# Two of eight chunk pairs of two merged down panels multiplied as 2x2 blocks with seven products

## The chip, the cores and the metric

One core of a Trainium2 chip runs the whole kernel. Its engines are TensorE (PE in the profile; its loads of the stationary operand are PEld), VectorE (DVE), ScalarE (ACT), GpSimd (POOL) and SyncE (SP, which issues the loads here). The metric is the device time of one execution in microseconds; the figure given for a kernel is the median of its runs.

## What is computed

A decoder trunk of two layers on 256 tokens of width 2048: a gated linear attention layer, then a forgetting attention layer, each with a memory attention head group and a channel mixer behind it. The change lies in the channel mixers:

```python
def conv_ffn(h, w_up, conv_w, conv_b, w_down):
    u = causal_dwconv(h @ w_up, conv_w, conv_b)
    a, val = split_cols(u, [FFN_HIDDEN, FFN_HIDDEN])
    return (jax.nn.silu(a) * val) @ w_down
```

`FFN_HIDDEN` is 5632, 44 chunks of 128; `w_down` is 5632 x 2048. All is fp32.

## The kernel before

**Precision.** Every fp32 operand is split into a high and a low part in fp32r, a = ah + al, and a product is ah·bh + al·bh + ah·bl, three matmuls. A weight comes as a *unit*: 128 x up to 1024 numbers (512 KB), loaded by SP into `raw`, cast by ScalarE into `whi` (L201), and VectorE subtracts to get `wlo` (L202). `raw`, `whi` and `wlo` have four buffers each. `split_unit` does this under `tc.high_priority(offset=AHEAD)`, AHEAD = 300: the scheduler, which fixes each engine's order when the kernel is built, treats it as if it stood 300 instructions earlier.

**The mixer.** `ffn` (L1186 on) works through three parts of the hidden chunks, `PARTS = ((0, 16), (16, 32), (32, 44))`. In each part the up panels (two chunks of the gate and two of the value each, eight units) are multiplied, their results turned through HBM and run through `convolve`, which leaves the product of SiLU and value in `m[i]`, split in high and low, chunk i as 128 hidden rows x 256 tokens. Then `add_out` multiplies `m` by the part's rows of `w_down`, in four panels f of 512 columns. A unit of a down panel holds two chunks x 512 columns; its 12 matmuls are 2 chunks x 2 token blocks b x 3 products, with 128 tokens of `m` stationary and 512 columns of the weight moving. The two token blocks accumulate in two PSUM banks, which VectorE adds into the residual `x[f]` (L330, `add_to`).

**The order of a part's down panels.** Panels 0 and 1 run through `two_tm`: seven units of panel 0, seven of panel 1, then the last unit of each; panel 1 accumulates in the two banks named `s`, panel 0 in two of the four named `acc`. Between these units the last convolutions are closed. Panels 2 and 3 then run one after the other through `proj_tm` (its matmul is L276), eight units each. Behind parts 0 and 1 follow the next part's up panels, behind part 2 the next stage of the trunk.

PSUM has eight banks here: four `acc`, two `s`, one `t`, one `o`.

Of the kernel before, what the change touches and what calls it, by code (L numbers as in the profile page):

```python
# [20 lines left out]
P = 128  # L21
# [17 lines left out]
NUNIT = 1024  # L39
AHEAD = 300  # L40
WARM = 9

FV_PARTS = ((0, 376), (376, 764), (764, 1152), (1152, 1536))

# [9 lines left out]
def _panels():  # L54

    full = list(range(KC))
    out = []

    def fm(key, w, c0, kcs=full):
        out.append((key, w, kcs, [(c0, 256)], 4))

    def tm(key, w, c0, n, kcs=full, more=()):
        out.append((key, w, kcs, [(c0, n), *more], 2))

    tm(("mv", 0), ("mem_w_kv", 0), 512, 512)
    for l in range(2):
        tm(("mk", l), ("mem_w_kv", l), 0, 512)
    tm(("mv", 1), ("mem_w_kv", 1), 512, 512)  # L70
    tm(("gv", 0), ("gla_w_in", 0), G_V, DV, more=[(G_R, RANK)])
    tm(("mq", 0), ("gla_w_in", 0), G_MQ, 512)
    for h in range(GLA_H):
        tm(("gqk", h), ("gla_w_in", 0), G_Q + h * DK, DK, more=[(G_K + h * DK, DK)])
        if h == GLA_H - 1:
            tm(("og", 0), ("gla_w_in", 0), G_OG, 512)
        if h:
            tm(("gv", h), ("gla_w_in", 0), G_V + h * DV, DV)
    for j in range(1, 3):
        tm(("og", j), ("gla_w_in", 0), G_OG + j * 512, 512)  # L80
    late = list(range(12, 16)) + list(range(12))

    def ffn(l):
        for p, (lo, hi) in enumerate(PARTS):
            for j in range(lo, hi, 2):
                tm(("up", l, j), ("ffn_w_up", l), j * P, 2 * P, more=[(HID + j * P, 2 * P)])
            for f in range(4):
                tm(("down", l, p, f), ("ffn_w_down", l), f * 512, 512, list(range(lo, hi)))

    for f in range(4):  # L90
        tm(("wo", 0, f), ("gla_w_out", 0), f * 512, 512, late)
# [12 lines left out]
    ffn(1)  # L104
    return out
# [30 lines left out]
def _trunk(ctx: ExitStack, tc: tile.TileContext, xt, xtok, memt, wp, wgu, gns, gfin, cnv, par, msk, out):  # L136
# [45 lines left out]
    def work(tag, bufs=1):  # L182
        return pwork.tile([P, 512], F32, name="ps_" + tag, tag=tag, bufs=bufs)
# [99 lines left out]
    def panel_tm(key, src, evac, second=False):  # L283

        units = where[key]
        n = units[0][2]
        base = min(min(u[1]) for u in units)
        acc = []  # L290
        end = len(units) - 1

        def step(i):
            if i == 0:
                acc.extend(work("s", 2) if second else pacc.tile([P, 512], F32, name="acc", tag="acc")
                           for _ in range(2))
            ready = split_unit(units[i])
            passes = [(b, low) for low in range(2) for b in range(2)]
            if i == end:
                passes.sort()  # L300
            for b, low in passes:
                for j, kc in enumerate(units[i][1]):
                    for part in range(2 - low):
                        mm = TE.matmul(acc[b][:, :n], src[kc - base][:, part, b * P : (b + 1) * P],  # L304
                                       ready[low][:, j * n : (j + 1) * n], start=i == low == part == j == 0,
                                       stop=i == end and low == 1 and j == len(units[i][1]) - 1)
                if i == end and low:
                    ends.append(mm)
                    evac(b, acc[b][:, :n])
            last_mm.append(mm)  # L310

        return step

    def run(step, hooks={}, count=8):

# [199 lines left out]
    def halves(dst, src):  # L515
        S.activation(dst[0], src, AF.Copy)
        V.tensor_tensor(dst[1], src, dst[0].bitcast(F32), ALU.subtract)
# [634 lines left out]
                    steps[f](u)  # L1152


    def add_out(key, src, then=None, spare=None, last=None, first=0, hooks=None, late=1):
# [13 lines left out]
        for f in range(first, 4):  # L1169
# [10 lines left out]
    def ffn(l, nx, h, m, ys, zs, landing, then, spare=None, last=None):  # L1180
        with tc.tile_pool(name=f"ffn{l}", bufs=1) as fp:
            cw = fp.tile([P, 4 * 88], F32, name="cw")
            nc.sync.dma_start(cw, cnv[l])
# [4 lines left out]
            count = [0, 0]  # L1188
            open_ = []

            def convolve(j, i, z):

                for s in range(2):
                    cv = {}
                    for c in range(2):
                        u = us[turn[0] % 4]
                        turn[0] += 1
                        V.tensor_tensor(by_run(u[:, 2:]), z[:, :, 2 * c + s], by_run(nx.row()), ALU.mult)  # L1198
                        col = (c * 44 + j + s) * 4
                        w = [cw[:, col + n : col + n + 1] for n in range(4)]  # L1200
                        r = fp.tile([P, T], F32, name=f"cv{c}", tag=f"cv{c}", bufs=3)
                        S.activation(r, u[:, 2:], AF.Identity, bias=w[3], scale=w[2])  # L1202
                        V.scalar_tensor_tensor(r, u[:, 1 : T + 1], w[1], r, ALU.mult, ALU.add)  # L1203
# [4 lines left out]
                    split(m, i + s, r)  # L1208

            def up(j, i, second=False):  # L1210

# [4 lines left out]
            def close(left):  # L1216

                while len(open_) > left:
                    j, i, back = open_.pop(0)
                    z = zs[count[1] % 2]  # L1220
                    count[1] += 1
                    with tc.issue_after(loads[-1].ins):
                        back(flat(z))
                    with tc.issue_after(lows[-1].ins):
                        convolve(j, i, z)

            for p, (lo, hi) in enumerate(PARTS):
                js = list(range(lo, hi, 2))
# [13 lines left out]
                        elif u == 2:  # L1242
                            close(1)
                end = p == len(PARTS) - 1
                down = {"then": then, "spare": spare, "last": last} if end else {}
                add_out(("down", l, p), m, hooks={(0, 2): lambda: close(1), (1, 4 if end else 3): lambda: close(0)}, **down)

    def preparing(name, dst, pool, far, kept=None, tag="blk"):

# [39 lines left out]
    with tc.tile_pool(name="stash", bufs=1) as st:  # L1289
        vt = st.tile([P, 2, FOX_H * HD], F32, name="fvt")  # L1290
        turned3 = vt.rearrange("p b t -> p (b t)").rearrange("p (f q k b j) -> p f q k b j", f=3, q=4, k=4, b=2)
        turned3 = [turned3[:, f] for f in range(3)]

        with tc.tile_pool(name="turn1", bufs=1) as tp:
            n2, then = preparing("kv", bufB, tp, dram, turned3)
            ys = [const.tile([P, 4, 4, 2, 32], F32, name="yu", tag=tag) for tag in ("mk0", "mv0")]
            ffn(0, n, bufB, bufA, ys, turned3, ys, then)
# [10 lines left out]
    with tc.tile_pool(name="store", bufs=1) as op:  # L1308
# [43 lines left out]
        ffn(1, n, bufA, bufB, ys, zs, zs, then, op, last)  # L1352


def _constants():
# [68 lines left out]
```

## Time and profile before

| what | value |
|---|---|
| median of 3 runs | 2238.03 us (2237.52 to 2239.8) |
| span of the profiled execution | 2235.5 us |
| TensorE matmuls | 10429, busy 2224.4 us |
| VectorE, ScalarE busy | 1587.6 us, 1181.8 us |

The profile is of one execution, taken by the chip's profiler; its span runs from the first to the last instruction, and the runs' times, taken without the profiler, also hold what lies around it: the median is 2.5 us above the span. The views used are the page's head, the waits (who waited for whom), the chain of work that ended last, windows (busy time of each engine in a stretch), groups of instructions by line and shape, and the timeline. A tile's name with an arrow, `wlo<-raw,whi`, is what is written and what is read. L12 is line 12 of the kernel.

### The profile page before, as it was taken

Reading aid. Unit: us, or ns where it says so; the run is one execution under the profiler, and the core shown is the slowest. Engines: PE = TensorE matmul, PEld = TensorE weight load, DVE = VectorE, ACT = ScalarE, POOL = GpSimd, SP = SyncE. Lnnn points to the kernel's source line nnn. Section 1 sums busy time; section 2 is a strip of 40 time slices with the busy share of each in tenths; the row PEclk is TensorE's granted clock in tenths of the full one; section 3 lists DMA queues with packets and bytes.
Section 4 is the critical chain, followed back from the end, with each engine's and each line's share of the span. In section 5 each row is a group of like instructions: output and inputs, shape, how many; then the busy total and the mean of one; then the engine's idle time right before and its main releaser. Section 6 shows DMA issues by size and latency. Waiting matters only on the chain.

```text
span 2235.5 us, 29529 instructions
## 1 busy us (share of the span) xinstructions
PE 2224.4 (100%) x10429; PEld 1874.1 (84%) x10429; DVE 1587.6 (71%) x2634; ACT 1181.8 (53%) x1751; POOL 3.4 (0%) x19
## 2 busy tenths in 40 slices
PE   9999999999999999999999999999999999999998
PEld 7888888888888888888888998888888888888886
DVE  7768977677775587656777569666877477765776
ACT  6655664555553455435565455454655355543554
POOL 0000000000000000000000000000000000000000
PEclk9999999999999999999999999999999999999999
DMA  9777667778876777667777767777876577766774
GB/s 353 227 220 226 193 188 244 246 236 245 248 227 196 227 241 244 211 200 233 245 247 247 216 194 244 232 239 255 248 239 220 193 236 244 238 204 210 241 244 142
DMA packets 183052, 513.33 MB, mean 230 GB/s; under 512 B 20588, under 2 KB 66296, under 8 KB 182776
## 3 DMA queue, kind: packets, MB, share of 16 engines
q1 hardware_dynamic: 182328, 510.66, 73.2%
q8 instruction: 81, 1.33, 0.2%
q10 hardware_dynamic: 576, 0.79, 0.1%
q14 instruction: 67, 0.55, 0.1%
HBM read 468.63 MB, written 42.74 MB: 229 GB/s over the span
## 4 chain that ended last, share of the span: by engine, by line
PE 98%; DMA 1%; DVE 1%; ACT 0%; SPq 0%; issue 0%; DVEq 0%
PE acc L304 70%; PE acc L276 13%; PE ps_s L304 9%; PE acc L232 3%; PE acc L230 1%; DMA fky<-far 0%; PE ps_s L854 0%; DMA raw<-wp 0%; PE ps_o L530 0%; PE ps_s L530 0%; PE ps_o L1072 0%; PE ps_s L1117 0%; PE ps_s L899 0%; DVE wlo L202 0%; PE ps_s L900 0%; PE ps_o L1074 0%
## 5 line engine op out<-in xcount | busy, mean ns | idle before, releaser
L202 DVE TENSOR_TENSOR wlo<-raw,whi 128x1024 fp32r<-128x1024 f32 (+4 forms) x809 | 969.2, 1200 | 576.7 <-ACT whi L201 559.7
L201 ACT ACTIVATE whi<-raw 128x1024 fp32r<-128x1024 f32 (+4 forms) x809 | 841.9, 1042 | 840.5 <-PE acc L304 534.2
L304 PE MATMUL acc<-whi,B 128*128 128x512 f32 (+3 forms) x2672 | 647.9, 380 | 0.0
L304 PEld LDWEIGHTS acc<-whi,B 128*128 128x128 f32 x2672 | 494.6, 188 | 83.4
L304 PE MATMUL acc<-whi,mix 128*128 128x512 f32 x1488 | 369.2, 390 | 0.0
L304 PE MATMUL acc<-wlo,B 128*128 128x512 f32 (+3 forms) x1336 | 352.9, 380 | 0.0
L304 PEld LDWEIGHTS acc<-whi,mix 128*128 128x128 f32 x1488 | 279.3, 188 | 57.8
L304 PEld LDWEIGHTS acc<-wlo,B 128*128 128x128 f32 x1336 | 248.4, 188 | 42.1
L304 PE MATMUL acc<-wlo,mix 128*128 128x512 f32 x744 | 200.5, 390 | 0.0
L304 PEld LDWEIGHTS acc<-wlo,mix 128*128 128x128 f32 x744 | 139.7, 188 | 28.8
L304 PE MATMUL acc<-whi,A 128*128 128x512 f32 x592 | 150.5, 389 | 0.0
L304 PEld LDWEIGHTS acc<-whi,A 128*128 128x128 f32 x592 | 111.2, 188 | 23.0
L276 PE MATMUL acc<-whi,mix 128*128 128x512 f32 x512 | 127.7, 390 | 0.0
L1202 ACT ACTIVATE cv<-u,cw 128x256 f32<-128x256 f32 x176 | 95.0, 591 | 58.8 <-DVE u L1198 57.6
L276 PEld LDWEIGHTS acc<-whi,mix 128*128 128x128 f32 x512 | 96.2, 188 | 20.0
L304 PE MATMUL ps_s<-whi,mix 128*128 128x512 f32 x336 | 83.8, 390 | 0.0
L304 PE MATMUL acc<-wlo,A 128*128 128x512 f32 x296 | 83.7, 390 | 0.0
L1204 DVE SCALAR_TENSOR_TENSOR cv<-u,cw,cv 128x256 f32<-128x256 f32 x176 | 77.9, 480 | 0.0
L1203 DVE SCALAR_TENSOR_TENSOR cv<-u,cw,cv 128x256 f32<-128x256 f32 x176 | 76.0, 474 | 0.0
L304 PEld LDWEIGHTS ps_s<-whi,mix 128*128 128x128 f32 x336 | 63.0, 188 | 13.0
L276 PE MATMUL acc<-wlo,mix 128*128 128x512 f32 x256 | 69.5, 390 | 0.0
L304 PEld LDWEIGHTS acc<-wlo,A 128*128 128x128 f32 x296 | 55.4, 188 | 11.4
(269 smaller groups left out, 1747.5 us busy)
## 6 DMA issues: line engine op xcount, KB each, us to landing
raw<-wp SPq DMA_DIRECT2D x743, 512.0 KB, 4.2
fvt<-far SPq DMA_DIRECT2D x100, 128.0 KB, 5.9
raw<-wp SPq DMA_DIRECT2D x32, 384.0 KB, 3.6
yzu<-far SPq DMA_DIRECT2D x96, 128.0 KB, 5.8
far<-yu SPq DMA_DIRECT2D x22, 512.0 KB, 2.7
far<-yzu SPq DMA_DIRECT2D x22, 512.0 KB, 2.8
raw<-wp SPq DMA_DIRECT2D x24, 388.0 KB, 3.9
far<-blk SPq DMA_DIRECT2D x12, 512.0 KB, 3.7
```

Source lines behind the costliest of these rows:

```text
L201: casts.append(S.activation(hi[:, s], raw[:, s], AF.Copy))
L202: lows.append(V.tensor_tensor(lo[:, s], raw[:, s], hi[:, s].bitcast(F32), ALU.subtract))
L230: mm = TE.matmul(acc[p][c][:, :T], w[:, s], both[:, 0, :], start=False, stop=end and j == 3)
L232: mm = TE.matmul(acc[p][c], w[:, s], both, start=u == j == 0, stop=end and j == 3)
L276: mm = TE.matmul(acc[b][:, :n], src[kcs[j] - base][:, part, b * P : (b + 1) * P], w, start=u == 0 and low == part == j == 0, stop=u == end ...
L304: mm = TE.matmul(acc[b][:, :n], src[kc - base][:, part, b * P : (b + 1) * P], ready[low][:, j * n : (j + 1) * n], start=i == low == part = ...
L1202: S.activation(r, u[:, 2:], AF.Identity, bias=w[3], scale=w[2])
L1203: V.scalar_tensor_tensor(r, u[:, 1 : T + 1], w[1], r, ALU.mult, ALU.add)
L1204: V.scalar_tensor_tensor(r, u[:, :T], w[0], r, ALU.mult, ALU.add)
```

## The change

In parts 0 and 1 of both mixers, panels 2 and 3 run as one, `pair_tm`. A unit is now one chunk x 1024 columns (panel 2's 512 and panel 3's 512), 16 units a part, in four open accumulations: two token blocks x two panels. The chunks of 0, 1 and 4, 5 (the pairs that begin with an index in `SEVEN`) are multiplied in block form. With A11 and A21 the two token blocks of the first chunk, A12 and A22 of the second, and B11, B12, B21, B22 the two panels' halves of the two chunks' weights, the seven products are

```
S1 = A21 + A22   S2 = S1 - A11   S3 = A11 - A21   S4 = A12 - S2
T1 = B12 - B11   T2 = B22 - T1   T3 = B22 - B12   T4 = B21 - T2
p1 = A11 B11     p2 = A12 B21    p3 = S4 B22      p4 = A22 T4
p5 = S1 T1       p6 = S2 T2      p7 = S3 T3
```

(A here is tokens x hidden, B hidden x columns.) `convolve` makes the S on VectorE and splits them (`sums`); `pair_tm` makes the T on VectorE from the raw weights and splits them. p2, p3, p4 accumulate straight into the banks that the plain units use for three of the four blocks; p1, p5, p6, p7 have the four `acc` banks and are put together behind the second group: one copy on ScalarE, three additions, and five additions into x. The packed weights are laid out to match, with 512 KB a unit as before. `add_out` gets a `count` of 2 in these parts. Extra tiles come from `room`: buffers of the pools around each mixer. Part 2 and everything outside the mixers is as before.

```diff
+SEVEN = (0, 4)
...
-            for f in range(4):
+            last = p == len(PARTS) - 1
+            for f in range(4 if last else 2):
                 tm(("down", l, p, f), ("ffn_w_down", l), f * 512, 512, list(range(lo, hi)))
+            for k in range(0 if last else hi - lo):
+                cols = [(1024, 512), (1536, 512)]
+                out.append((("pair", l, p, k), ("ffn_w_down", l), [lo + k], cols[:: -1 if k in SEVEN else 1], 1))
...
+    def split_more(src, n):
+
+        with tc.high_priority(offset=AHEAD):
+            hi = wpool.tile([P, NUNIT], F32R, name="whi", tag="whi", bufs=4)
+            lo = wpool.tile([P, NUNIT], F32R, name="wlo", tag="wlo", bufs=4)
+            casts.append(S.activation(hi[:, :n], src, AF.Copy))
+            lows.append(V.tensor_tensor(lo[:, :n], src, hi[:, :n].bitcast(F32), ALU.subtract))
+        return hi, lo
...
+    def pair_tm(units, src, sums, room, out):
...
+        for name, tag in (("p1", "acc"), ("p2", "o"), ("p3", "s"), ("p5", "acc"), ("p7", "acc"), ("p6", "acc"), ("p4", "s"),
+                          ("x", "t")):
+            new(name, tag)
...
+        def mm(name, x, w, last):
+            for i, (a, b) in enumerate(((0, 0), (1, 0), (0, 1))):
+                r = TE.matmul(bank[name], x[a], w[b], start=name not in begun, stop=last and i == 2)
...
+            if kind == "plain":
+                w = split_unit(units[k])
+                last = k == n - 1
+                for low in range(2):
+                    for name, b, h in (("p2", 0, 0), ("p3", 0, 1), ("p4", 1, 0), ("x", 1, 1)):
+                        for part in range(2 - low):
+                            r = TE.matmul(bank[name], tok(k, b)[part], w[low][:, h * 512 : (h + 1) * 512],
+                                          start=name not in begun, stop=last and low == 1)
...
+            else:
+                ra, rb = load_unit(units[k]), load_unit(units[k + 1])
+                b12, b11, b21, b22 = ra[:, :512], ra[:, 512:], rb[:, :512], rb[:, 512:]
+                st = [[sums[k][:, part, j, :] for part in range(2)] for j in range(4)]
+                done = i == end
+                w = split_more(b11, 512)
+                mm("p1", tok(k, 0), [t[:, :512] for t in w], done)
+                w = split_more(rb, 1024)
+                mm("p2", tok(k + 1, 0), [t[:, :512] for t in w], False)
+                mm("p3", st[3], [t[:, 512:] for t in w], False)
+                with tc.high_priority(offset=AHEAD):
+                    ta, tb = room("t"), room("t")
+                    V.tensor_tensor(ta[:, :512], b12, b11, ALU.subtract)
+                    V.tensor_tensor(ta[:, 512:], b22, b12, ALU.subtract)
+                    V.tensor_tensor(tb[:, :512], b22, ta[:, :512], ALU.subtract)
+                    V.tensor_tensor(tb[:, 512:], b21, tb[:, :512], ALU.subtract)
+                w = split_more(ta, 1024)
+                mm("p5", st[0], [t[:, :512] for t in w], done)
+                mm("p7", st[2], [t[:, 512:] for t in w], done)
+                w = split_more(tb, 1024)
+                mm("p6", st[1], [t[:, :512] for t in w], done)
+                last_mm.append(mm("p4", tok(k + 1, 1), [t[:, 512:] for t in w], False))
+                if done:
+                    one, two = room("e")
+                    three = room("f")
+                    S.activation(one, bank["p1"], AF.Copy)
+                    V.tensor_tensor(two, bank["p6"], one, ALU.add)
+                    V.tensor_tensor(three, bank["p7"], two, ALU.add)
+                    V.tensor_tensor(two, bank["p5"], two, ALU.add)
+                    out(0, 1, two)
+                    out(1, 1, three)
+                    out(1, 1, bank["p5"])
+                    out(1, 0, three)
+                    out(0, 0, one)
+        ends.append(r)
+        for name, b, h in (("p2", 0, 0), ("p3", 0, 1), ("p4", 1, 0), ("x", 1, 1)):
+            out(b, h, bank[name])
...
+                if seven:
+                    (a11, a21), (a12, _) = [[r[:, b * P : (b + 1) * P] for b in range(2)] for r in rs]
+                    a22 = rs[1][:, P:]
+                    t = room("s")[:, :512].rearrange("p (j n) -> p j n", j=4)
+                    V.tensor_tensor(t[:, 0, :], a21, a22, ALU.add)
+                    V.tensor_tensor(t[:, 1, :], t[:, 0, :], a11, ALU.subtract)
+                    V.tensor_tensor(t[:, 2, :], a11, a21, ALU.subtract)
+                    V.tensor_tensor(t[:, 3, :], a12, t[:, 1, :], ALU.subtract)
+                    sums[i] = room(i)
+                    halves([sums[i][:, part] for part in range(2)], t)
...
-                        convolve(j, i, z)
+                        convolve(j, i, z, j < PARTS[-1][0] and i in SEVEN)
...
-                down = {"then": then, "spare": spare, "last": last} if end else {}
+                down = {"then": then, "spare": spare, "last": last} if end else {"count": 2}
...
+                if not end:
+                    units = [where[("pair", l, p, k)][0] for k in range(hi - lo)]
+                    pair_tm(units, m, sums, room, lambda b, h, a: add_to(2 + h)(b, a))
```

More of the change, by code (lines that the diff above doesn't have):

```diff
@@ L312, in panel_tm, with load_unit @@
         return step
+    def split_more(src, n):
[5 more added lines that the diff above has]
+        return hi, lo
+    def load_unit(unit):
+        off, kcs, n = unit
+        w = len(kcs) * n
+        with tc.high_priority(offset=AHEAD):
+            raw = wpool.tile([P, NUNIT], F32, name="raw", tag="raw", bufs=4)
+            loads.append(nc.sync.dma_start(raw[:, :w], wp[off : off + P * w].rearrange("(p n) -> p n", p=P)))
+        return raw
@@ new lines, in pair_tm, with new, tok @@
+    def pair_tm(units, src, sums, room, out):
+        bank = {}
+        def new(name, tag):
+            bank[name] = pacc.tile([P, 512], F32, name="acc", tag="acc") if tag == "acc" else work(tag, 2 if tag == "s" else 1)
+        for name, tag in (("p1", "acc"), ("p2", "o"), ("p3", "s"), ("p5", "acc"), ("p7", "acc"), ("p6", "acc"), ("p4", "s"),
+                          ("x", "t")):
+            new(name, tag)
+        begun = set()
+        n = len(units)
+        plan = []
+        k = 0
+        while k < n:
+            if k in SEVEN:
+                plan.append(("seven", k))
+                k += 2
+            else:
+                plan.append(("plain", k))
+                k += 1
+        end = [i for i, (kind, _) in enumerate(plan) if kind == "seven"][-1]
+        def mm(name, x, w, last):
+            for i, (a, b) in enumerate(((0, 0), (1, 0), (0, 1))):
+                r = TE.matmul(bank[name], x[a], w[b], start=name not in begun, stop=last and i == 2)
+                begun.add(name)
+            return r
+        def tok(k, b):
+            return [src[k][:, part, b * P : (b + 1) * P] for part in range(2)]
+        for i, (kind, k) in enumerate(plan):
+            if kind == "plain":
[6 more added lines that the diff above has]
+                                          start=name not in begun, stop=last and low == 1)
+                            begun.add(name)
+                last_mm.append(r)
+            else:
+                ra, rb = load_unit(units[k]), load_unit(units[k + 1])
[7 more added lines that the diff above has]
+                mm("p3", st[3], [t[:, 512:] for t in w], False)
+                with tc.high_priority(offset=AHEAD):
+                    ta, tb = room("t"), room("t")
[24 more added lines that the diff above has]
+            out(b, h, bank[name])
@@ L1152, in fox, with add_out @@
                     steps[f](u)
-    def add_out(key, src, then=None, spare=None, last=None, first=0, hooks=None, late=1):
+    def add_out(key, src, then=None, spare=None, last=None, first=0, hooks=None, late=1, count=4):
         def evac_of(f):
@@ L1168, in add_out @@
                    len(where[(*key, 0)]), late, hooks)
-        for f in range(first, 4):
+        for f in range(first, count):
             if f == 3 and hasattr(then, "land"):
@@ L1178, in add_out, with ffn @@
                 proj_tm((*key, f), src, last if f == 3 and last is not None else evac_of(f), spare if f == 3 else None)
-    def ffn(l, nx, h, m, ys, zs, landing, then, spare=None, last=None):
+    def ffn(l, nx, h, m, ys, zs, landing, then, room, spare=None, last=None):
         with tc.tile_pool(name=f"ffn{l}", bufs=1) as fp:
@@ L1189, in ffn, with convolve @@
             open_ = []
-            def convolve(j, i, z):
+            sums = {}
+            def convolve(j, i, z, seven):
+                rs = []
                 for s in range(2):
@@ L1208, in convolve @@
                     split(m, i + s, r)
+                    rs.append(r)
+                if seven:
[8 more added lines that the diff above has]
+                    halves([sums[i][:, part] for part in range(2)], t)
             def up(j, i, second=False):
@@ L1296, in _trunk, with room @@
             ys = [const.tile([P, 4, 4, 2, 32], F32, name="yu", tag=tag) for tag in ("mk0", "mv0")]
-            ffn(0, n, bufB, bufA, ys, turned3, ys, then)
+            def room(kind):
+                if kind in ("t", "s"):
+                    return tp.tile([P, NUNIT], F32, name="tsum", tag="blk", bufs=2)
+                if kind == "e":
+                    return [tp.tile([P, 512], F32, name=f"ev{i}", tag=f"ev{i}") for i in range(2)]
+                if kind == "f":
+                    return tp.tile([P, 512], F32, name="ev2", tag="ev2")
+                return tp.tile([P, 2, 4, P], F32R, name="asum", tag=f"asum{kind}")
+            ffn(0, n, bufB, bufA, ys, turned3, ys, then, room)
         fox(n2, vt, turned3)
@@ L1351, in _trunk, with room @@
         ys, zs = ([const.tile([P, 4, 4, 2, 32], F32, name="yzu", tag=f"{t}{i}") for i in range(2)] for t in ("mk", "mv"))
-        ffn(1, n, bufA, bufB, ys, zs, zs, then, op, last)
+        def room(kind):
+            if kind in ("t", "s"):
+                return op.tile([P, NUNIT], F32, name="tsum", tag="wlo", bufs=3)
+            if kind == "e":
+                t = op.tile([P, NUNIT], F32, name="ev", tag="whi", bufs=3)
+                return t[:, :512], t[:, 512:]
+            if kind == "f":
+                return op.tile([P, 512], F32, name="ev2", tag="ev2")
+            return op.tile([P, 2, 4, P], F32R, name="asum", tag="whi", bufs=3)
+        ffn(1, n, bufA, bufB, ys, zs, zs, then, room, op, last)
 def _constants():
```

## The prediction

> **What bounds the kernel now.** I read the page first, then who waited for whom on TensorE, then the chain of waits around the stage that is changed.
>
> ```profile
> span 2235.5 us, 29529 instructions
> PE 2224.4 (100%) x10429; PEld 1874.1 (84%) x10429; DVE 1587.6 (71%) x2634; ACT 1181.8 (53%) x1751; POOL 3.4 (0%) x19
> ...
> PEclk9999999999999999999999999999999999999999
> ```
> ```profile
> PE ps_o L176 <- DVE B L173: 1.4, 1, 1.4
> PE acc L276 <- ACT whi L201: 0.7, 1, 0.7
> PE ps_t L440 <- DVE dg L438: 0.2, 1, 0.2
> ```
>
> TensorE is busy throughout at full clock, and in all of the run it waits 2.3 us for others (columns: total, times, longest). So only fewer or shorter matmuls make this kernel shorter, and another engine counts only if it makes TensorE wait. The chain of waits shows the stage that changes: down panels 2 and 3 of the first two parts, in both layers, all by L276 (columns: start, length, count).
>
> ```profile
> 675.79 43.52 PE acc L276 x192
> ...
> 936.91 43.52 PE acc L276 x192
> ...
> 1725.95 43.52 PE acc L276 x192
> ...
> 1987.07 43.52 PE acc L276 x192
> ```
>
> Four stages of 192 matmuls, each without a gap: 43.52/192 = 226.67 ns a matmul. Beside it, by windows (columns: stretch, its length, then busy time and count of PE, PEld, DVE, ACT, POOL, then clock, DMA share, GB/s), the first such stage, the stage behind it, and the up panel in which VectorE is fullest:
>
> ```profile
> 675.79:719.31 43.52, 43.52 (x194) 36.06 (x193) 22.17 (x20) 16.98 (x17) 0.00 (x0) 1.00 0.62 195
> 719.31:763.00 43.69, 43.69 (x195) 36.19 (x194) 23.00 (x24) 17.63 (x18) 0.00 (x0) 1.00 0.69 217
> ...
> 523.50:545.20 21.70, 21.70 (x97) 17.97 (x97) 18.69 (x33) 12.21 (x19) 0.00 (x0) 1.00 0.78 243
> ```
>
> VectorE is at 51% of the changed stage, ScalarE at 39%. Both have room; whether it lies at the right moment is what the prediction turns on.
>
> **The change part by part: matmuls.** Before, a unit (two chunks, 512 columns) is 12 matmuls, 16 units 192. After, a plain unit (one chunk, 1024 columns) is 4 blocks x 3 = 12 again, and a group of two chunks in block form is 7 products x 3 = 21 instead of 24. A stage has 12 plain units and 2 groups: 144 + 42 = 186. All keep 512 moving columns and a 128x128 stationary block. Removed: 6 a stage, 24 in all, 24 x 226.67 ns = **5.44 us**. Nothing else leaves TensorE's queue.
>
> **Order of banks.** Plain units now change the PSUM bank after two matmuls with the high half and after one with the low half, 8 changes in 12 where L276 has 4. The trace has one projection that changes the bank at every matmul, L232:
>
> ```profile
> 1342.23 6.16 PE acc L232 x27
> ```
> ```profile
> 1342.20:1348.40 6.20, 6.20 (x30) 5.12 (x29) 6.20 (x17) 4.66 (x10) 0.00 (x0) 1.00 0.88 309
> ```
>
> 6.16/27 = 228.1 ns, 1.5 ns above L276. L232 also swaps the operands' roles (the weights are stationary there), so the 1.5 ns need not be the banks. Ends: 0, and 1.5 ns on all 4 x 186 = 744 matmuls = 1.1 us. In a straight line between 4 and 12 changes, 8 would give 0.75 ns on the 576 plain matmuls = 0.4 us; as the roles may explain it all, I take half, **0.2 us**. The groups change banks 7 times in 21, as rarely as L276: 0.
>
> One rule of the Trainium skill speaks against this part. Its page "TensorE: Matmul & The Clock Gate" (section "A second HAM failure mode: psum-queue depth-cycling") tells of a kernel that cycled through the PSUM banks each iteration, micro-idled between its groups and had its clock drop to half and back. The window of L232 disagrees so far: bank after bank, clock 1.00.
>
> **What VectorE and ScalarE get.** The prices (columns: group, count | busy, mean ns of one | idle before):
>
> ```profile
> L202 DVE TENSOR_TENSOR wlo<-raw,whi 128x1024 fp32r<-128x1024 f32 x743 | 906.5, 1222 | 531.1 <-ACT whi L201 520.5 <-PE acc L276 4.4 <-PE acc L230 2.7
> L202 DVE TENSOR_TENSOR wlo<-raw,whi 128x512 fp32r<-128x512 f32 x2 | 1.4, 690 | 3.3 <-ACT whi L201 3.3
> L1317 DVE TENSOR_TENSOR x<-x,gf 128x512 f32<-128x512 f32 x6 | 4.1, 686 | 0.1
> L807 DVE TENSOR_TENSOR gk<-gqk,gd 128x128 f32<-128x128 f32 x4 | 1.2, 291 | 0.0
> L201 ACT ACTIVATE whi<-raw 128x1024 fp32r<-128x1024 f32 x743 | 786.3, 1059 | 780.8 <-PE acc L304 480.8 <-PE acc L276 130.3 <-PE ps_s L304 69.5
> L201 ACT ACTIVATE whi<-raw 128x512 fp32r<-128x512 f32 x2 | 1.2, 622 | 1.1 <-DMA raw<-wp 1.1
> ```
>
> - A group: one split of 512 and three of 1024 columns, and four subtractions of 512. VectorE 0.69 + 3 x 1.22 + 4 x 0.69 = 7.1 us, ScalarE 0.62 + 3 x 1.06 = 3.8 us, against 21 x 0.2267 = 4.76 us of TensorE. Inside a group VectorE is 2.35 us short.
> - A plain unit: 1.22 us against 2.72 us, as before.
> - Behind the second group: one ScalarE copy, three adds and five additions into x on VectorE, 8 x 0.69 = 5.5 us; at the stage's end four more, 2.8 us, where panels 2 and 3 had four of them too.
> - Stage on VectorE: 12 x 1.22 + 2 x 7.1 + 5.5 + 2.8 = 37.1 us of 186 x 0.2267 = 42.2 us, 88%. It fits; the question is the queue at the two groups.
> - In two convolutions of a part: four 128x128 sums (4 x 0.29) and a split of 512 (0.69), 1.9 us on VectorE, 0.6 us on ScalarE. Cover: the fullest panel has 21.7 - 18.69 = 3.0 us free, and the weights' splits run ahead of this work. Late next would be the sums, first read over 100 us afterwards. 0 us; without that cover 8 x 1.9 = 15 us.
>
> **Does the group come in time?** The timeline of TensorE, ScalarE and VectorE ahead of the first stage (start, length):
>
> ```profile
> 666.81 1.06 ACT L201 ACTIVATE whi<-raw 128x1024 fp32r<-128x1024 f32 x1 [1.66 <-PE ps_s L304]
> ...
> 667.91 1.23 DVE L202 TENSOR_TENSOR wlo<-raw,whi 128x1024 fp32r<-128x1024 f32 x1 [1.50 <-ACT whi L201]
> ...
> 669.53 1.06 ACT L201 ACTIVATE whi<-raw 128x1024 fp32r<-128x1024 f32 x1 [1.66 <-PE ps_s L304]
> ...
> 670.63 1.23 DVE L202 TENSOR_TENSOR wlo<-raw,whi 128x1024 fp32r<-128x1024 f32 x1 [1.50 <-ACT whi L201]
> ...
> 671.77 0.68 DVE L330 TENSOR_TENSOR x<-x,acc 128x512 f32<-128x512 f32 x1
> ...
> 672.66 1.06 ACT L201 ACTIVATE whi<-raw 128x1024 fp32r<-128x1024 f32 x1 [2.06 <-PE acc L304]
> ...
> 673.75 1.23 DVE L202 TENSOR_TENSOR wlo<-raw,whi 128x1024 fp32r<-128x1024 f32 x1
> ...
> 674.89 0.68 DVE L330 TENSOR_TENSOR x<-x,ps_s 128x512 f32<-128x512 f32 x1
> ...
> 675.38 1.06 ACT L201 ACTIVATE whi<-raw 128x1024 fp32r<-128x1024 f32 x1 [1.66 <-PE ps_s L304]
> 675.41 1.77 PEld L276 LDWEIGHTS acc<-whi,mix 128*128 128x128 f32 x8
> 675.63 1.98 PE L276 MATMUL acc<-whi,mix 128*128 128x512 f32 x8
> 675.83 0.69 DVE L330 TENSOR_TENSOR x<-x,ps_s 128x512 f32<-128x512 f32 x1 [0.26 <-PE ps_s L304]
> 676.47 1.23 DVE L202 TENSOR_TENSOR wlo<-raw,whi 128x1024 fp32r<-128x1024 f32 x1
> ```
>
> Each cast waits for TensorE to free one of four buffers, so four units are split ahead: the casts from 666.81 on serve what TensorE takes up from 675.8 on. In the changed kernel these four buffers go to B11, (B21, B22), the first pair of subtractions and the second.
>
> - VectorE stands idle for 1.50 us ahead of 670.63, and the raw blocks landed long before, so the four subtractions (2.7 us) can mostly run at 668.6 to 671.2. The low half of (B21, B22) is then done at about 672.4; products p2 and p3 need it from 676.5 + 0.45.
> - The third buffer is cast at 672.66, its low half done at 675.0; p5 needs it at 677.8.
> - The fourth is cast at 675.38, low half done at 677.7; p6 needs it at 679.2. Margin 1.5 us.
> - The first plain unit behind it waits for B11's buffer (free at 676.3): low half at 678.9, needed at 680.6. Margin 1.7 us. The second: 680.1 against 683.3.
> - Second group, from 686.0: casts at 679.0, 680.4, 682.4 and 685.1, low halves by 680.8, 682.7, about 685.9 and 687.4; the last is needed at 689.4. Margin 2 us.
> - The 5.5 us behind it find the splits three units ahead again (the unit needed at 696 is split by about 691.5), and these go first.
>
> By this no group makes TensorE wait: **0 us**. Banks: a stage uses all eight, and the one that comes late is p3's, freed by the addition of 674.89 to 675.6; p3 starts at 677.2. The waits added on the load queue:
>
> ```profile
> DMA to landing us min/median/max: 2.8/4.1/9.3
> ```
> ```profile
> SPq L196 <- DVE wlo L202: 1033.5, 542, 8.4
> ```
>
> A raw block is held until its last subtraction (676 at the latest) rather than its low half, and the load that takes its place waits with the loads behind it on SP. 676 + 4.1 = 680.1 for the second group's blocks, whose casts come at 679.0 and 680.4 and whose first product starts at 686.0: 0 us at the median; a landing of 9.3 us would be at 685.3, and about 1.5 us would be lost once.
>
> **Sum.** 2235.5 - 5.44 + 0.2 = 2230.3 us of span. The median of the runs is 2238.03, 2.5 us above the span, for what lies around it: **2232.8 us**, 0.23% below.
>
> **Rivals.**
> - *Matmuls of the new order are dearer.* All 744 run at L232's rate: +1.1 us instead of 0.2, 2233.7 us, -0.19%. For: L232. Against: its operands differ.
> - *The groups are fed late at the stage's start.* If the scheduler puts the subtractions behind the low half of (B21, B22), VectorE has from 671.9 on four subtractions, four additions into x and three splits in one row; the addition that frees p3's bank then ends at about 677.9 instead of before 677.2, 0.7 us lost. Four times: 2.8 us, 2235.6 us; at all eight groups 5.6 us, 2238.4 us. For: 88% load. Against: 1.5 us margins and idle time ahead of 670.63.
> - *VectorE becomes the bound, and the kernel slower.* From B11 of the first group to the last split of the second it has 2 x 7.1 + 2 x 1.22 + 4 x 0.69 = 19.4 us against 2 x 4.76 + 2 x 2.72 = 15.0 us. With the lead of four buffers used up (half-filled buffers cover 4.76 us of TensorE where full ones cover 10.9), 4.4 us a stage, 17.8 us: 2250.6 us. It decides once 2.5 us a stage are lost (9.9 us in all). For: group and unit order leave two plain units to catch up, and the order of VectorE's queue is set when the kernel is built. Against: B11's low half would be ready at 668.6, 7.2 us ahead of its use.
> - *The change saves no matmul time because the block form stalls at each of its many short accumulations*: no row shows a cost at a bank change in L276; this is the first rival at a higher price and goes with it.
> - By the page's clock rule, named above, half clock over the four stages would add up to 744 x 226.67 ns = 168.6 us: 2401 us. The trace's 1.00 under L232 leaves it 1 in 100.
>
> **How the numbers follow.** About 0.2%, 4.5 us, is what a measurement of this kernel can tell from no change (2233.55 to 2242.5 us). Forecast 0.56, own range 2231.5 to 2233.5 (matmul price 0, or half of the excess and a stray wait; static orders elsewhere may shift by some tenths); it counts as faster, but for 0.06 of it where stray waits of 0.8 us eat the small margin over 0.2%. Dearer matmuls 0.08, same. Fed late 0.18, same. VectorE the bound 0.17, slower. Clock 0.01, slower. So faster 0.50, same 0.32, slower 0.18. Lowest time: no price at all, 5.44 us off, 2232.6, less 1 us for a shifted order elsewhere: 2231.5. The upper end takes in late feeding at all eight groups and the stray load, 2238.4 + 1.5 = 2240; left out is VectorE as the bound and the clock.
>
> **What would show it.** The four stages in the chain: 186 matmuls in 42.2 us each, or, with dearer matmuls, 42.4. TensorE's waits stay near 2.3 us; waits on whi or wlo inside the groups, or on an L330 addition ahead of p3, show late feeding and its size. VectorE at about 88% of the stage. PEclk 9 in all slices. The prediction is wrong if TensorE waits more than 1 us a stage for splits, or if time changes outside the four stages.

## The result and the profile after

| | before | after |
|---|---|---|
| median of 21 runs | 2237.11 us | 2233.5 us |
| lowest, highest | 2236.29, 2240.39 us | 2231.77, 2236.02 us |
| span of the profiled execution | 2235.5 us | 2231.5 us |

The ratio of after to before is 0.9984, with a 95% interval from 0.9977 to 0.999: 0.16% faster, 3.6 us between the medians, where 2232.8 us and 0.23% were forecast. (The 2238.03 us that the forecast started from is the median of the first three of these 21 runs.) By the 0.2% that a measurement of this kernel was taken to tell from no change, the gain lies a little short of "faster"; its interval leaves out zero.

First the page of the changed kernel, then who waited for whom on TensorE (total, times, longest):

```profile
span 2231.5 us, 29658 instructions
...
PE 2220.2 (99%) x10405; PEld 1869.1 (84%) x10405; DVE 1647.4 (74%) x2754; ACT 1200.5 (54%) x1779; POOL 3.4 (0%) x19
```
```profile
PE ps_o L182 <- DVE B L179: 1.4, 1, 1.4
PE ps_t L545 <- DVE dg L543: 0.8, 1, 0.8
PE acc L282 <- ACT whi L207: 0.2, 1, 0.2
```

24 matmuls fewer (10429 to 10405), and no wait of TensorE inside a group: nothing on L363 (the groups) or L377 (the plain units). The wait for `dg`, a tile in front of the forgetting attention, has grown from 0.2 to 0.8 us; the change doesn't touch that place.

The four merged stages by windows, cut where the chain of waits has their first and last matmul (stretch, length, then busy time and count of PE, PEld, DVE, ACT, POOL, then clock, DMA share, GB/s):

```profile
675.73:718.12 42.39, 42.39 (x187) 34.94 (x187) 31.27 (x35) 21.35 (x22) 0.00 (x0) 1.00 0.62 200
935.72:978.11 42.39, 42.39 (x188) 34.93 (x187) 31.44 (x35) 21.35 (x22) 0.00 (x0) 1.00 0.62 201
1724.16:1766.57 42.41, 42.41 (x187) 34.92 (x187) 31.91 (x36) 21.46 (x22) 0.00 (x0) 1.00 0.64 200
1984.17:2026.57 42.40, 42.40 (x187) 34.91 (x187) 31.98 (x36) 21.50 (x22) 0.00 (x0) 1.00 0.62 200
```

They took 4 x 43.52 = 174.08 us and take 169.59 us: 4.49 us saved, not 5.44. The rest of the span: 0.56 us given back at the wait for `dg`, 0.07 us gained at the start. 4.49 - 0.56 + 0.07 = 4.0 us, the difference of the spans.

How the first group runs, by the timelines of VectorE and TensorE (start, length):

```profile
663.55 0.69 DVE L393 TENSOR_TENSOR tsum<-raw 128x512 f32<-128x512 f32 x1
...
673.74 1.23 DVE L326 TENSOR_TENSOR wlo<-tsum,whi 128x1024 fp32r<-128x1024 f32 x1
...
677.13 0.68 DVE L435 TENSOR_TENSOR x<-x,ps_s 128x512 f32<-128x512 f32 x1
677.73 1.22 DVE L326 TENSOR_TENSOR wlo<-tsum,whi 128x1024 fp32r<-128x1024 f32 x1
```
```profile
676.93 1.10 PE L363 MATMUL acc<-whi,asum 128*128 128x512 f32 x4
677.87 0.62 PE L363 MATMUL acc<-wlo,asum 128*128 128x512 f32 x2
678.33 0.64 PE L363 MATMUL ps_s<-whi,asum 128*128 128x512 f32 x2
678.80 0.40 PE L363 MATMUL ps_s<-wlo,asum 128*128 128x512 f32 x1
679.03 0.63 PE L363 MATMUL acc<-whi,asum 128*128 128x512 f32 x2
679.50 0.62 PE L377 MATMUL ps_o<-whi,mix 128*128 128x512 f32 x2
...
681.32 0.40 PE L363 MATMUL acc<-wlo,asum 128*128 128x512 f32 x1
```

The subtractions (`tsum<-raw`) start 12 us ahead of the stage. The last low half of the group starts at 677.73 and is done at 679.0. TensorE doesn't want it then: between p6's high half (679.03) and its low half (681.32) the scheduler has put high halves of the next plain unit. The stages take 42.39 to 42.41 us where 186 x 226.67 ns is 42.16 us, 0.12 us more a group. The distances from start to start show where most of it goes: the first four matmuls on `asum`, the tile of the sums S, take 677.87 - 676.93 = 0.94 us, 235 ns each, where a plain one takes 227. Over the whole trace two matmuls on `asum` in a row start 233 ns apart on average.

### The profile page after: what moved, and what is told of

Same layout as the page of the kernel before. It is cut to its first block, busy times and chain, and to the rows that moved or that the text cites. A ratio compares the mean times of both kernels' runs of the same rounds, so it can differ in the third digit from the quotient of the medians.

```text
span 2231.5 us, 29658 instructions
## 1 busy us (share of the span) xinstructions
PE 2220.2 (99%) x10405; PEld 1869.1 (84%) x10405; DVE 1647.4 (74%) x2754; ACT 1200.5 (54%) x1779; POOL 3.4 (0%) x19
## 4 chain that ended last, share of the span: by engine, by line
PE 98%; DMA 1%; DVE 1%; ACT 0%; SPq 0%; issue 0%; DVEq 0%
PE acc L310 71%; PE ps_s L310 9%; PE acc L282 5%; PE ps_s L377 3%; PE acc L238 3%; PE ps_o L377 1%; PE ps_t L377 1%; PE acc L236 1%; PE acc L363 1%; PE ps_s L363 0%; PE ps_s L959 0%; DMA fky<-far 0%; DMA raw<-wp 0%; PE ps_o L635 0%; PE ps_s L635 0%; PE ps_o L363 0%
## 5 line engine op out<-in xcount | busy, mean ns | idle before, releaser
L208 DVE TENSOR_TENSOR wlo<-raw,whi 128x1024 fp32r<-128x1024 f32 (+4 forms) x793 | 948.2, 1198 | 502.5 <-ACT whi L207 483.4
L207 ACT ACTIVATE whi<-raw 128x1024 fp32r<-128x1024 f32 (+4 forms) x793 | 825.1, 1042 | 781.7 <-PE acc L310 504.2
L310 PE MATMUL acc<-whi,mix 128*128 128x512 f32 x1488 | 369.0, 389 | 0.0
L310 PEld LDWEIGHTS acc<-whi,mix 128*128 128x128 f32 x1488 | 279.2, 188 | 57.9
L310 PE MATMUL acc<-wlo,mix 128*128 128x512 f32 x744 | 200.4, 390 | 0.0
L1314 ACT ACTIVATE cv<-cv 128x256 f32<-128x256 f32 x88 | 36.7, 418 | 35.3 <-DVE cv L1312 31.7
L310 PE MATMUL ps_s<-whi,B 128*128 128x512 f32 x208 | 52.5, 389 | 0.0
L238 PE MATMUL acc<-mix,whi 128*128 128x512 f32 x192 | 48.9, 394 | 0.0
```

Of the source, the lines that this page charges most:

```text
L207: casts.append(S.activation(hi[:, s], raw[:, s], AF.Copy))
L208: lows.append(V.tensor_tensor(lo[:, s], raw[:, s], hi[:, s].bitcast(F32), ALU.subtract))
L238: mm = TE.matmul(acc[p][c], w[:, s], both, start=u == j == 0, stop=end and j == 3)
```

## The experiments

Each was compared with the kernel before on the same chip; its medians there were 2236.6 to 2237.3 us.

**The order alone.** No group, only the merged panels:

```diff
-SEVEN = (0, 4)
+SEVEN = ()
```

(The four banks of p1, p5, p6, p7 are not taken either.)

> The merged stage with no group in block form: 16 plain units, 192 matmuls a stage, the new order of banks alone. Theory (only the number of matmuls counts, the order of banks is free, and the excess of 0.23 us a stage seen in the changed kernel belongs to the groups): each of the four stages takes 192 x 226.67 ns = 43.52 us again, the time is that of the kernel before within 0.1%, about 2237 us. Rival (the new order of banks is dearer, as in L232): 1.5 ns on 768 matmuls, stages of 43.8 us and 2238.3 us. If the longer wait of TensorE in front of the forgetting attention (0.8 us instead of 0.24) comes from the merged order, it shows here too.

2236.96 us, ratio 0.9999 (0.999 to 1.0007). The first stage:

```profile
675.63:719.15 43.52, 43.52 (x194) 36.04 (x193) 20.72 (x19) 17.32 (x17) 0.00 (x0) 1.00 0.60 195
```

192 matmuls at 226.67 ns. Changing the bank eight times in twelve costs nothing here, and the excess belongs to the groups. The wait for `dg` is absent here.

**Three groups, four groups.**

```diff
-SEVEN = (0, 4)
+SEVEN = (0, 4, 8)
...
-                    return [tp.tile([P, 512], F32, name=f"ev{i}", tag=f"ev{i}") for i in range(2)]
+                    t = tp.tile([P, NUNIT], F32, name="ev", tag="blk", bufs=2)
+                    return t[:, :512], t[:, 512:]
                 if kind == "f":
-                    return tp.tile([P, 512], F32, name="ev2", tag="ev2")
+                    return tp.tile([P, NUNIT], F32, name="ev2", tag="blk", bufs=2)[:, :512]
```

The second part makes room in SBUF for the third group's S. Four groups (0, 4, 8, 12) need more of it: `ev2` of the second mixer shares a buffer too, the fourth S there has a tile of its own, and the convolution's tiles `cv0` and `cv1` have two buffers instead of three.

> Three groups a stage (chunks 0, 4 and 8), the three tiles of the final sums moved into the buffers of the subtractions to make room. Theory (TensorE's count sets the time while VectorE has room): 36 matmuls fewer than before = 8.16 us, less 12 groups x 0.12 us of excess and 0.6 us at the forgetting attention: 2237.1 - 8.16 + 1.4 + 0.6 = 2230.9 us. VectorE, by the spacing of its instructions in the changed kernel (1.14 us a split, 0.6 us a subtraction or sum), needs 10 x 1.14 + 3 x 6.4 + 7.2 = 37.8 us of 41.5 us. Rival (VectorE's lead is used up by two groups): no better than two groups, 2233.5 us or more, with waits of TensorE on whi and wlo in the third group.

> Four groups a stage (chunks 0, 4, 8 and 12); to make room the final sums share buffers as in the kernel with three, and the convolution's tiles have two buffers instead of three. Theory (count alone): 48 matmuls fewer = 10.88 us, less 16 x 0.12 us and 0.6 us: 2228.7 us. Rival (VectorE becomes the bound here): 8 x 1.14 + 4 x 6.4 + 7.2 = 41.9 us of VectorE against 180 x 0.2267 = 40.8 us of TensorE a stage, and the sums of the last group fall into the stage's end; TensorE waits 1 us or more a stage, 2233 us or more.

> The kernel with four groups again, unaltered, for more runs of what was the fastest: a median of 2228 to 2230 us, stages of 41.3 us, and TensorE's wait for dg somewhere between 0 and 2 us. If its first median (five runs) was luck, it comes out nearer to that of three groups, 2230.5 us.

Three groups: 2230.5 us, ratio 0.9966 (0.9952 to 0.9979). Four groups: 2228.68 us, 0.9961 (0.9949 to 0.9974), and in the second set of five runs 2227.74 us, 0.996 (0.9946 to 0.9974), a little below the 2228 to 2230 us expected. Count alone holds for both. The first stage with three groups, and with four:

```profile
675.19:717.01 41.82, 41.82 (x185) 34.38 (x184) 35.14 (x41) 23.05 (x24) 0.00 (x0) 1.00 0.61 203
```
```profile
675.64:716.94 41.30, 41.30 (x181) 33.81 (x181) 36.38 (x42) 24.47 (x26) 0.00 (x0) 1.00 0.58 199
```

183 and 180 matmuls would be 41.48 and 40.80 us: 0.11 and 0.12 us of excess a group again, so a group is worth 3 x 226.67 ns - 0.12 us = 0.56 us. VectorE is busy 84% and 88% of the stage, and TensorE waits for none of it. Four groups beat both kernels, the one before by 8.1 us in the first set and 9.5 us in the second (2236.82 to 2228.68 and 2237.28 to 2227.74).

**The subtractions at plain priority.** This was meant to take their lead away:

```diff
-                with tc.high_priority(offset=AHEAD):
+                with tc.high_priority(offset=0):
                     ta, tb = room("t"), room("t")
```

> The changed kernel with the four subtractions of a group at plain priority instead of 300 instructions ahead; all else as it is. Theory (the lead is the cover that hides them): they fall behind the splits, the third and fourth buffers of a group are late, and TensorE waits 0.7 to 4.4 us a stage: 2236 to 2251 us. Rival (VectorE has idle time ahead of each group in any case, and the scheduler fills it): 2233.5 us, unchanged.

2232.71 us, ratio 0.998 (0.9971 to 0.9989): unchanged. But the edit moved nothing. The first subtraction of the first group is again 12 us ahead of the stage (663.55 in the changed kernel):

```profile
663.15 0.69 DVE L393 TENSOR_TENSOR tsum<-raw 128x512 f32<-128x512 f32 x1
...
676.88 1.22 DVE L326 TENSOR_TENSOR wlo<-tsum,whi 128x1024 fp32r<-128x1024 f32 x1
```

All instructions of VectorE, ScalarE and TensorE stand in the same order in the two traces. The splits that need the subtractions still stood 300 instructions ahead; whether that is why the order stayed is not shown. So this is the changed kernel once more, and what the lead is worth stays untested.

**More work on VectorE.** Every subtraction twice (`for _ in range(2)` around the four), with two groups and with four:

> The changed kernel (two groups) with every subtraction done twice: 8 more instructions of 0.6 us on VectorE a stage, 4.8 us, on 31.3 to 32 us of 42.4 us. Theory (VectorE has room, and a group is served from idle time ahead of it): unchanged, 2233.5 us, stages of 42.4 us. Rival (the margins of 1.5 to 2 us that the prediction worked out are all there is, and 2.4 us more a group use them up): TensorE waits 0.4 to 0.9 us a group, 8 groups, 2237 to 2241 us.

> Four groups a stage with every subtraction done twice: 16 more instructions of 0.6 us on VectorE a stage, 9.6 us. VectorE was busy 36.4 of 41.3 us with four groups, so 46.0 us against 41.3 us. Theory (VectorE becomes the bound once its work exceeds the stage): TensorE waits for splits inside the groups, 2 to 5 us a stage, 2237 to 2248 us. Rival (idle VectorE time ahead of the stage takes most of it, as scheduling is free to move it): less than 1 us a stage, under 2233 us.

Two groups: 2233.8 us, ratio 0.9984 (0.9975 to 0.9993), the same as with each done once. Stages take 42.46 to 42.66 us instead of 42.4, so 2.4 us more a group cost at most 0.13 us a group. Four groups: 2248.68 us, ratio 1.0048 (1.0031 to 1.0065). There VectorE is the bound, as TensorE's waits and the windows of the first two stages show, in which VectorE is busy 97% and 96% of the time. Below them stand windows around the last groups of the third stage, and one in the fourth:

```profile
PE acc L363 <- ACT whi L325: 9.3, 15, 1.3
...
PE acc L363 <- DVE wlo L326: 1.0, 2, 0.8
```
```profile
675.52:719.54 44.02, 43.10 (x186) 34.26 (x184) 42.85 (x52) 23.30 (x26) 0.00 (x0) 1.00 0.54 176
936.23:981.49 45.26, 43.30 (x185) 34.19 (x184) 43.46 (x53) 23.55 (x26) 0.00 (x0) 1.00 0.56 177
...
1748.00:1752.60 4.60, 3.11 (x13) 1.89 (x11) 4.48 (x6) 2.13 (x3) 0.00 (x0) 1.00 0.57 195
1752.60:1756.10 3.50, 3.46 (x9) 2.73 (x10) 2.65 (x3) 2.79 (x4) 0.00 (x0) 0.57 0.55 177
...
1762.00:1766.60 4.60, 3.10 (x14) 1.88 (x12) 3.46 (x6) 2.67 (x4) 0.00 (x0) 1.00 0.43 125
1766.60:1770.30 3.70, 3.70 (x9) 2.95 (x10) 3.70 (x4) 3.70 (x4) 0.00 (x0) 0.54 0.53 151
...
2032.99:2036.40 3.41, 3.41 (x9) 2.68 (x9) 3.41 (x4) 3.03 (x4) 0.00 (x0) 0.50 0.53 187
```

The waits are for casts of `tsum`, which wait for the subtractions. They add to 10.3 us, while the span is 2246.6 - 2225.9 = 20.7 us longer than with four groups and single subtractions. Part of the difference is the clock: behind a window in which TensorE was busy 3.1 of 4.6 us, the granted clock is 0.57 and 0.54 over some 3.5 us, and 0.50 in the last row. These three stretches are the only ones inside the four stages. Counted from start to start of the matmuls, the pauses take 16.0 us and the half clock 4.6 us, which together is the difference; the 10.3 us are less because a matmul's record ends 0.39 us after its start, while the next can start after 0.23. The time lies just above the range expected.

**Where the excess comes from.** Left out in turn: the S as stationary operand, the subtractions T, and the values of S.

```diff
-                st = [[sums[k][:, part, j, :] for part in range(2)] for j in range(4)]
+                st = [tok(k, 0), tok(k, 1), tok(k + 1, 0), tok(k + 1, 1)]
```
```diff
-                with tc.high_priority(offset=AHEAD):
-                    ta, tb = room("t"), room("t")
-                    V.tensor_tensor(ta[:, :512], b12, b11, ALU.subtract)
...
+                ta, tb = ra, rb
```
```diff
-                    V.tensor_tensor(t[:, 0, :], a21, a22, ALU.add)
+                    V.tensor_tensor(t[:, 0, :], a11, a11, ALU.max)
...
```

(The third copies A11, A21, A12 and A22 into the tile of the S.)

> Left out: the products with the sums S use the chunks themselves as stationary blocks instead of S (the S are still made). Same 186 matmuls a stage, same splits and subtractions, only the stationary tile differs. The changed kernel's stages take 42.39 to 42.41 us where 186 x 226.67 ns = 42.16 us, an excess of 0.12 us a group. Theory A (the excess comes with the tile of the S, which is read as stationary operand): stages of 42.16 to 42.2 us. Rival B (it comes with the order of the group, its many short runs of matmuls on freshly split weights, or with the subtractions beside it): stages of 42.4 us as before. Time within 1 us of 2233.5 us either way.

> Left out: the four subtractions T of a group; the raw weight blocks are split and multiplied in their place. Same matmuls and splits. If VectorE's subtractions beside the group cause the excess of 0.12 us a group, the stages fall to 42.16 us; if the group's order or the S tile does, they stay at 42.4 us. If the subtractions cost TensorE nothing, as the prediction had it, the time stays within 1 us of 2233.5 us.

> Left out: the sums S; the four blocks of A are copied into the same tile by four instructions of the same shape, so the products of a group read the tile of the S, but with the values that the kernel with the chunks as stationary blocks used (its stages were 42.16 us). Theory A1 (reading that tile costs the 0.12 us a group: its place or its making): stages of 42.4 us. Theory A2 (the values of the S cost it): stages of 42.16 us.

The first stage of the first and of the third kernel:

```profile
674.93:717.09 42.16, 42.16 (x188) 34.91 (x187) 31.32 (x35) 21.34 (x22) 0.00 (x0) 1.00 0.63 201
```
```profile
675.44:717.84 42.40, 42.40 (x188) 34.97 (x187) 31.36 (x35) 21.35 (x22) 0.00 (x0) 1.00 0.63 199
```

With the chunks themselves as stationary blocks, and TensorE's matmuls in the same order as in the changed kernel, all four stages take 42.16 us, 186 x 226.67 ns to the last digit. With the same values read from the tile of the S they take 42.39 to 42.41 us. Without the subtractions they stay at 42.36 to 42.39 us. So the excess comes with that tile, not with its values, nor with VectorE's subtractions. Whether its place in SBUF, its layout or the way it is written does it wasn't tried. One particular place is unlikely: `room` gives the S tiles buffers of other pools in the second mixer than in the first, and the excess there is the same (stages of 42.41 and 42.40 us). One run of each took 2231.51, 2235.96 and 2232.27 us; the first two miss the 1 us around 2233.5 that was expected. The first lacks the 0.95 us of excess and reaches its first stage 0.8 us earlier (674.93 against 675.73); the second has the longest wait for `dg` of all, and behind it 3.42 us at half clock, at most another 1.7 us:

```profile
PE ps_t L540 <- DVE dg L538: 2.2, 1, 2.2
```
```profile
1206.04:1209.46 3.42, 3.42 (x10) 2.67 (x10) 3.42 (x8) 1.69 (x2) 0.00 (x0) 0.50 0.38 149
```

**The changed kernel once more.**

> The changed kernel once more, unaltered: a second profile of the same program. TensorE's wait for dg in front of the forgetting attention was 0.24 us before, 0.8 us after, 0 to 1.9 us in the variants. If it hangs on the landing of the last turned block (fky), which differs from one execution to the next, it comes out different from 0.8 us here, with the span moved by the same amount from 2231.5 us and the four stages unchanged at 42.4 us. If the change's static order sets it, it is 0.8 us again.

2233.83 us, span 2232.1 us; the stages are the same and the wait for `dg` is longer:

```profile
PE ps_t L545 <- DVE dg L543: 1.3, 1, 1.3
```

The chain of waits names the load of the last turned block, first in the first profile of the changed kernel, then in this one:

```profile
1189.96 9.50 DMA fky<-far
```
```profile
1191.04 8.94 DMA fky<-far
```

It lands at 1199.46 and at 1199.98, 221.35 and 221.85 us behind the end of the second stage (978.11 and 978.13). The landing is 0.5 us later in the second and so is the wait. In the kernel before it landed at 1191.37 + 9.82 = 1201.19, 220.76 us behind that stage's end at 980.43: 0.59 us earlier than in the first profile after, and there the wait was 0.56 us shorter. The kernel with the subtractions at plain priority, whose order is the same, agrees: its load lands 1.06 us later than in the first profile after, and the wait is 1.9 us, 1.1 us longer. One order of instructions has waits of 0.8, 1.3 and 1.9 us, so this is how executions differ; over all the profiles of the case the wait runs from 0 (order alone and four groups among them) to 2.2 us.

## Why the prediction was right, and where its sizes were off

- **Matmuls.** Right: TensorE's count sets the time of the stages, at a period that depends on the stationary tile. 186 a stage, 24 fewer, 5.44 us at the period of the rows; with the chunks as stationary blocks the stage showed it exactly.
- **Order of banks, 0.2 us, up to 1.1.** Wrong in cause. Eight changes in twelve are free (43.52 us with the order alone, where the straight line has 0.75 ns on each matmul), so L232's 1.5 ns are hardly its banks, and the straight line drawn to them meant nothing. The mis-sized term is another one that the sum took as 0, the matmuls of the groups: 0.23 to 0.25 us a stage, 0.95 us in all, for the tile of the S as stationary operand. I had priced a stationary block as one price whatever tile it is read from.
- **VectorE, 37.1 us of 42.2.** Too high: 31.3 to 32 us, 74 to 75%. Part of the group's work runs ahead of the stage (the first subtraction at 663.55), most of the last four additions run behind its end, and a split of 1.22 us holds the next one up for 1.14 us only: in a queue the spacing counts.
- **In time, 0 us.** Right, though not by the order worked out. The low half of the third buffer fell where it was put, at 673.74 (the row of before has 673.75); the fourth's ended at 679.0, 1.3 us later than the 677.7 worked out, behind the addition at 677.13, which stands at 675.83 in the rows of before. What the hand-made order missed is that the scheduler also moves matmuls: high halves of other products stand between p6's halves, which moves the need for the fourth buffer's low half from 679.7 to 681.3. So 2.3 us were left, where the hand-made order would have left 0.7. Twice the subtractions cost at most 0.13 us a group.
- **The idle time ahead of the group as cover.** The subtractions did run in it, earlier than worked out. Whether they need their lead in the queue for that is open, as the run that was to take it away kept the order.
- **Rivals.** Dearer matmuls, held at 0.08, is the rival whose sign came: stages of 42.4 us, and 2233.5 us where it gave 2233.7. Its reason, L232 and the banks, was wrong; it is the tile of the S. Late feeding did not happen. VectorE as the bound is real, but lies beyond four groups: four with single subtractions are free of waits at 88% of the stage, four with double ones lose 20 us. With two groups it was far off: doubling the subtractions there made TensorE wait for nothing. Half clock from the new order of banks did not come either: the granted clock is 1.00 in all four stages.
- **The sum.** 4.49 us at the stages; 0.56 us went to the wait for `dg`, which differs between executions of one order. By its own words the prediction would be wrong if time changed outside the four stages, and there it did; what speaks for chance is that spread of 0.8 to 1.9 us. Whether the change moves the average of this wait is not shown: the medians are 3.6 us apart, and the interval of the ratio, 2.2 to 5.1 us, takes in 4.49. The forecast's 0.23% needed nearly all of the 5.44 us; the measured saving lies 0.9 us short of the 0.2% bound, about what the S tile took.
- **The 2.5 us around the span.** Too large, and it brought luck. It set the median of three runs against the span of another execution. Where the record has time and span of one execution they are 1.7 to 2.1 us apart (2233.26 and 2231.5 us for the profiled run after). Span against span, 2230.3 us was forecast and 2231.5 measured: 1.2 us of the saving were missing. With 1.8 us in place of the 2.5 the forecast would have been 2232.1 us, 1.4 us below the measured 2233.5; that it is only 0.7 us below is luck.

## What to carry to other kernels

In a kernel that its TensorE bounds from end to end, trading matmuls for vector work pays by its count, less what the new operands cost (0.95 of 5.44 us here), until the other engine's queue is full. What sets how far it can go may be memory: here room in SBUF for the S tiles had to be made for a third and fourth group, and each group was worth 0.56 us. Judge the other engine by the spacing of its instructions over the stage and the stretch ahead of it, not by the sum of their durations inside the stage. Before calling a variant a test, see in its trace that the order it was to change has changed. When a gain is near what can be measured, read it from the lengths of the changed stages, and look for a transfer elsewhere whose landing moves the total by as much.

## What the runs showed that was not expected

A matmul with the tile of the S as stationary operand takes about 233 ns from start to start where one on the chunks takes 227, with the same values, form and clock. The groups of the changed kernel's first stage show it in their durations too (count | busy, mean ns; the ends of matmuls are modelled in this profile), p3's high halves, the dearest, against those of a plain unit:

```profile
L377 PE MATMUL ps_o<-whi,mix 128*128 128x512 f32 x16 | 4.9, 390 | 0.0
...
L363 PE MATMUL ps_s<-whi,asum 128*128 128x512 f32 x4 | 1.3, 400 | 0.0
```

Short waits can cost twice. With four groups and double subtractions no wait was longer than 1.3 us, and yet the clock fell to about half. The timeline of TensorE there (the waits in brackets):

```profile
1751.18 1.20 PE L363 MATMUL acc<-whi,asum 128*128 128x512 f32 x4 [1.26 <-ACT whi L325]
1752.64 0.85 PE L363 MATMUL acc<-whi,asum 128*128 128x512 f32 x2 [0.26 <-ACT whi L325]
1753.28 1.05 PE L363 MATMUL ps_s<-whi,B 128*128 128x512 f32 x2
1754.14 1.05 PE L363 MATMUL acc<-wlo,asum 128*128 128x512 f32 x2
```

From 1753.28 to 1754.14 two matmuls take 0.86 us, 430 ns each instead of 227. The single wait of 2.2 us for `dg` above was followed by half clock too, while waits of 1.9 us (subtractions at plain priority) and 1.7 us (three groups) for the same tile were not. The Trainium skill ("TensorE: Matmul & The Clock Gate", section "Part 1: The HAM clock gate") ties the return to half clock to an idle window of about 3.4 us. With the double subtractions the longest wait is 1.3 us, and TensorE was busy 3.11 of the 4.60 us ahead; the measurement decides, and a kernel should not count on short waits being free of it.
